# Hybrid encoder trunk: transposes, gating and split of the delta rule's output as a stage of their own ahead of w_out's products, and one gate chunk moved behind the Hyena norm

## Chip, cores and metric

The kernel runs on one core of a Trainium2 chip. The metric is the device time of one execution in microseconds. Five engines work side by side, each through an in-order queue of its own: TensorE (PE, matrix products), VectorE (DVE), ScalarE (ACT), GpSimd (POOL) and SyncE (SP, which issues nearly all the loads). Semaphores order the queues among each other.

## Reference

Two layers over 256 tokens of width 1024; all arrays are float32.

```python
for i in range(2):
    x = x + 0.5 * swiglu(rmsnorm(x), gate1, up1, down1)          # 1024 -> 2816 -> 1024
    q, k, v, z, beta, alpha, hy = split(rmsnorm(x) @ w_in)
    o_dn = rmsnorm_per_head(delta(q, k, v, ...) + flipped_delta(...)) * silu(z)   # 4 heads x 128
    o_hy = rmsnorm(x2 * longconv(x1 * longconv(v)))              # 512 channels
    x = x + concat([o_dn, o_hy]) @ w_out                         # 1024 x 1024
    x = x + 0.5 * swiglu(rmsnorm(x), gate2, up2, down2)
return rmsnorm(x)
```

The change touches the end of the mixer (the third to sixth line of the loop): the norm and the gate `silu(z)` of the delta rule's output, the Hyena norm, and the product with w_out.

## Kernel before

**Layout.** x is kept transposed: 8 tiles of 128 channels by 256 tokens. A feed-forward block walks over 22 steps of 128 hidden channels, each with three weight blocks of 512 KB (gate, up, down). The mixer makes its inputs in 28 chunks of 128 channels (`chunk`), the last four being the gate z.

**Split weights.** Products with the feed-forward weights and with w_out run in a reduced 32-bit format on operands that are split into a high and a low half. `load_w` lets SP load a block into a `raw` buffer (4 of them), ACT copies the high half into `wh` (3 buffers, line 179), DVE subtracts to give the low half `wl` (3 buffers, line 182). `split_act` does the same with activations (`yp`: ACT line 152, DVE line 153). `rank` multiplies one block of w_out (128 of its 1024 rows) by such a pair: three products for each of 8 output tiles, 24 in all, added into four PSUM banks (`acc`, tags c and d). The z chunks are not split: `load_raw` loads the weights, and a product of full float32 takes 8 products of two passes each. They read `yn`, a float32 copy of the normalised input, which lives in one `wl` and one `wh` buffer until the last chunk has read it.

**The end of the mixer, in program order.** Stage z makes the four gate tiles `zs` (`chunk(24 + i, ..., Silu)`, ACT line 530). Stage hn multiplies back the last long convolution (`py`), squares, sums (`st`), and ends with `hn.finish()`: `nv` (DVE), a power on POOL (`pw`, line 195), `dg` (DVE), `rbp` (PE), `rb` (ACT). Stage hw scales the Hyena rows by `rb` (`yn`, DVE line 942), splits them and runs `rank` on w_out's blocks 4 to 7. Stages solve and o finish the delta rule: products `ph`, then `po`; a sum of squares (`oss`), a power on POOL and a product on DVE give the normalised output `on` (line 960), one tile for each half of the tokens. Stage ow, for each of four heads, transposes the head's two 128 x 128 pieces into a PSUM tile `pot` (line 1002; tag b, 2 banks, shared with `st`, `rbp` and the z chunks' `pw`), gates it (`og`, DVE line 1004), splits it and runs `rank` on w_out's blocks 0 to 3. Stage ef loads and splits the first four weight blocks of the next feed-forward block (`early`; high half on ACT, low half on POOL, line 182), and `finish_resid` adds `acc` to x.

**What sets the order.** The program order is not the order on the engines. A planner goes through a modelled execution when the program is built, and on each engine takes, among the instructions that are ready, the one with the lowest place number. That is its place in the program, less an offset: `stage(name)` takes the offset from the table `PRM` (solve 800, o 800; z, hn, hw and ow have none; ef has -410), and some groups have one of their own inside a stage (`nfin` 350 in the norm's end, `feed` and `feedw` 300 for the loads and splits of weights, `evac` 2060). A tile also waits in the plan for a free buffer of its tag. The order that results is fixed; on the chip each engine keeps to it.

Of the kernel before, what the change touches and what calls it, by code (L numbers as in the profile page):

```python
# [55 lines left out]
PRM = { 'split': list(range(28, 36)),  # L56
 'y32': 300,
 'ah': [0, 0, 0],
 'av': 0,
 'ak': 0,  # L60
 'aq': 0,
 'gm_act': [1, 3],
 'e_lc': [0, 1, 0, 1, 0, 0, 0, 0, 0, 1],
 'e_both': [1, 1],
# [7 lines left out]
 'w1': 6,  # L72
 'sqp0': [1, 2, 4, 5, 7],
 'hold': 3,
 'ej': 0,
 'ea': ['S', 'e4', 'e2', 'e2', 'd2', 'd2', 'zg', 'ST'],
 'fj': 14,
# [12 lines left out]
def trunk_kernel(ctx: ExitStack, tc: tile.TileContext, xt, ffn, wba, win, wout, par, fpar, fwo, fnorm, con, feat, wnd, out):  # L90
# [10 lines left out]
    def pr(name):  # L101
        n = PRM.get(name, 0)
        return tc.high_priority(offset=n) if n else nullcontext()
# [6 lines left out]
    def stage(name):  # L110
        cur.close()
        cur.enter_context(pr(name))

    def psum(tag, name, shape=(128, 4, 128)):
        return ps.tile(list(shape), F32, tag=tag, name=name, bufs=2)

    def mm(o, l, r, start=True, stop=True, **kw):
        PE.matmul(o, lhsT=l, rhs=r, start=start, stop=stop, **kw)  # L118
# [24 lines left out]
    def behind(i, j):  # L143

        tc.add_manual_dep(i.ins, j.ins.name, mybir.DependencyInfo(mybir.DependencyClass.NoSync, mybir.DependencyReason.DATA), reason="order")

    def split_act(src, tag, bufs, scale=None, eng=V):

        pair = ap_.tile([128, 2, T], F32R, tag=tag + "p", name=tag + "p", bufs=bufs)
        hi, lo = pair[:, 0], pair[:, 1]  # L150
        if scale is None:
            A.activation(out=hi, in_=src, func=AF.Copy)  # L152
            eng.tensor_tensor(out=lo, in0=src, in1=hi.bitcast(F32), op=ALU.subtract)  # L153
        else:
            last[0] = A.activation(out=hi, in_=src, func=AF.Copy, scale=scale)
            last[1] = PRM["hold"]
            eng.scalar_tensor_tensor(out=lo, in0=src, scalar=scale, in1=hi.bitcast(F32), op0=ALU.mult, op1=ALU.subtract)  # L157
        return hi, lo, pair

    def cut(pieces, c):  # L160
        z = pieces[0].shape[1]
        return pieces[c.start // z][:, c.start % z:c.start % z + c.stop - c.start]

    def load_w(src, n=1024, eng=V, tag="", bufs=3, early=None):
        raw = wp.tile([128, n], F32, tag=tag + "raw", name="raw", bufs=bufs + (tag == ""))
        SP.dma_start(out=raw, in_=src)
        if early is None:
            hi = [wp.tile([128, n], F32R, tag=tag + "wh", name="wh", bufs=bufs)]
            lo = [wp.tile([128, n], F32R, tag=tag + "wl", name="wl", bufs=bufs)]
        else:  # L170
            t = [mx.tile([128, c], F32R, tag=g, name="early", bufs=b) for g, c, b in early]
            if len(t) == 1:
                t = [t[0][:, 0:1024], t[0][:, 1024:2048]]
            hi, lo = t[:len(t) // 2], t[len(t) // 2:]
        ns = max(len(hi), PRM["wsp"] if n == 1024 else 1)
        for i in range(ns):
            c = slice(i * n // ns, (i + 1) * n // ns)
            h, l_ = cut(hi, c), cut(lo, c)
            op = A.activation(out=h, in_=raw[:, c], func=AF.Copy)  # L179
            if last[1] > 0 and early is None and n == 1024:  # L180
                behind(op, last[0])
            eng.tensor_tensor(out=l_, in0=raw[:, c], in1=h.bitcast(F32), op=ALU.subtract)  # L182
        last[1] -= 1
        return hi, lo
# [109 lines left out]
    def accumulators(tags="aadd"):  # L294
        banks = [psum(t, "acc", (128, 2, T)) for t in tags]
        return [banks[m // 2][:, m % 2] for m in range(KD)]
# [19 lines left out]
    def load_raw(src):  # L316
        raw = wp.tile([128, 1024], F32, tag="raw", name="raw", bufs=4)
        SP.dma_start(out=raw, in_=src)
        return raw
# [5 lines left out]
    def rank32(acc, w, h, first, last):  # L325
        for m in range(KD):
            mm(acc[m], w[:, m * 128:(m + 1) * 128], h, start=(first and m % 2 == 0), stop=last, skip_group_check=True)
# [8 lines left out]
    def rank(acc, w, h, first, last):  # L336

        for m in range(KD):
            for i, (a, b) in enumerate(((0, 0), (1, 0), (0, 1))):
                mm(acc[m], cut(w[a], slice(m * 128, (m + 1) * 128)), h[b], start=(first and i == 0 and m % 2 == 0), stop=(last and i == 2),  # L340
                   skip_group_check=True)
# [161 lines left out]
    def bh(apc):  # L503

        return apc.unsqueeze(2).to_broadcast([128, 4, 128])

    def mixer(l, ys, norm, ab, wcols):
# [5 lines left out]
        def chunk(c, dst=None, func=AF.Copy):  # L513
            with pr("feed"):
                if early:
                    w = early.pop(0)
                else:
                    w = load_w(win[l, c]) if c in PRM["split"] else load_raw(win[l, c])
            p = psum("bc"[c % 2] if c < 4 else "b", "pw", (128, T))
            raw = ap_.tile([128, T], F32, tag="t1", name="raw_", bufs=7) if dst is None else dst  # L520
            if isinstance(w, tuple):
                proj(p, w, ys)
                with pr("evac"):
                    V.tensor_tensor(out=raw, in0=p, in1=norm.rb, op=ALU.mult)
                    if func != AF.Copy:
                        after(A.activation(out=raw, in_=raw, func=func), last_exp)
            else:
                proj32(p, w, yn)
                with pr("evac"):
                    i = A.activation(out=raw, in_=p, func=func)  # L530
                    if func != AF.Copy:
                        after(i, last_exp)
            return raw
# [41 lines left out]
        def tok(name, bufs):  # L575
            return [mx.tile([128, CW], F32, tag=name, name=name, bufs=bufs) for _ in range(2)]

        def d2(name):
            return mx.tile([128, 4, 128], F32, tag="d2", name=name, bufs=8)
# [130 lines left out]
        for a in range(2):  # L710
            for hp in (slice(0, 2), slice(2, 4)):
                p = psum("a", "gram", (128, 2, 2, 128))
                for i in range(2):
                    h = hp.start + i
                    mm(p[:, i], kq[:, h, 0, a * 128:(a + 1) * 128], kq[:, h, 0])
                for i in range(2):
                    h = hp.start + i
# [18 lines left out]
        for a in range(2):  # L736
            both, one = ((Ef0, Eb[0, 0]), (Eb1, Ef[1, 1]))[a]
            for hp in (slice(0, 2), slice(2, 4)):
                p = psum("d", "kqp", (128, 2, 2, 128))
                for i in range(2):  # L740
                    h = hp.start + i
# [8 lines left out]
        for q_ in range(4):  # L750
            t = d2("xm")
# [54 lines left out]
        for i in range(4):  # L806
            t = ap_.tile([128, T], F32, tag="hc", name="hv", bufs=4)
# [42 lines left out]
        for i in range(4):  # L850
            t = mx.tile([128, T], F32, tag="zs", name="vs", bufs=4)
# [4 lines left out]
        for a in range(2):  # L856
# [3 lines left out]
            t = d2("rho")  # L860
# [6 lines left out]
        for i in range(4):  # L867
            t = ap_.tile([128, T], F32, tag="hc", name="h1", bufs=4)
# [4 lines left out]
        z1 = tok("zt", 2)  # L873
# [38 lines left out]
        for i in range(4):  # L912
            t = ap_.tile([128, T], F32, tag="hc", name="x2", bufs=4)
# [2 lines left out]
        stage("z")  # L916

        zs = []
        for i in range(4):
            t = mx.tile([128, T], F32, tag="zs", name="zs", bufs=4)  # L920
            chunk(24 + i, t, AF.Silu)
            zs.append(t)

        stage("hn")
        hn = Norm(4, CW, "b")
        for i in range(4):
# [6 lines left out]
            V.tensor_tensor(out=xv, in0=py, in1=xv, op=ALU.mult)  # L933
            hn.add(x2[i])
        hn.finish()

        stage("hw")

        acc = accumulators("ccdd")
        for i in range(4):  # L940
            t = ap_.tile([128, T], F32, tag="t1", name="yn", bufs=7)
# [3 lines left out]
            else:  # L945
                with pr("feedw"):
                    w = load_w(wout[l, 4 + i])
# [10 lines left out]
        def tt(name, x, y, op):  # L958
            t = d2(name)
            V.tensor_tensor(out=t, in0=x, in1=y, op=op)  # L960
            return t
# [23 lines left out]
        for i in range(2):  # L985
# [9 lines left out]
            V.scalar_tensor_tensor(out=ss, in0=ss, scalar=1.0 / 128, in1=ssq[:, 4 * i:4 * i + 4], op0=ALU.mult, op1=ALU.add)  # L995
            f = rsqrt(ss, 4, f"of{i}")
            on.append(tt("on", po, bh(f), ALU.mult))
        stage("ow")
        for h in range(4):
            pt = psum("b", "pot", (128, T))  # L1000
            for i in range(2):
                PE.transpose(pt[:, i * 128:(i + 1) * 128], on[i][:, h], ident)
            t = ap_.tile([128, T], F32, tag="t1", name="og", bufs=7)
            V.scalar_tensor_tensor(out=t, in0=pt, scalar=P[:, C_DNN:C_DNN + 1], in1=zs[h], op0=ALU.mult, op1=ALU.mult)
            if 32 + h not in PRM["split"]:
                rank32(acc, load_raw(wout[l, h]), t, False, h == 3)
            else:
                with pr("feedw"):
                    w = load_w(wout[l, h])
                rank(acc, w, split_act(t, "y", 8), False, h == 3)  # L1010
        stage("ef")
        for _ in ahead([ffn[l, 1, j, i] for j in range(2) for i in range(2)], PRM["ma"]):
            pass
# [140 lines left out]
```

## Time and profile before

| | |
|---|---|
| median of 3 runs | 1235.63 us (1233.08 to 1235.89) |
| the profiled execution, its own time | 1238.01 us |
| span of the profiled execution, first to last instruction | 1236.2 us |
| mean granted clock of TensorE | 0.989 of 2.4 GHz |
| busy: PE, DVE, ACT, POOL | 1191.8, 867.8, 588.1, 304.8 us |
| transposes `pot`, first and last start | 393.8 and 1014.6 us |
| gate tiles `zs`, first and last start | 363.0 and 986.5 us |

The profile is of one execution. A start is counted from the span's first instruction; a row that says x4 merges four instructions that follow each other, with the time from the first start to the last end. Times in brackets behind a row are idle time of that engine just before it, with what ended it. PE's clock column is the granted share of 2.4 GHz. The two mixers lie at about 225 to 430 us and 830 to 1035 us of the span, with the same order of instructions.

### The profile page before, as it was taken

What the parts mean: (1) busy time and instruction counts of PE and PEld (TensorE: products, weight loads), DVE (VectorE), ACT (ScalarE), POOL (GpSimd) and SP (SyncE); (2) the same over time, 40 slices, a digit from 0 to 9 for tenths busy, and PEclk for the clock granted to TensorE, in tenths of its full rate; (3) what the DMA queues carried; (4) which work ended last, traced back from release to release, by engine and by line L of the source; (5) the groups of instructions that cost most, each with busy time, mean ns of one, the idle gap of its engine ahead of it and who ended that gap; (6) DMA issues with size and microseconds to landing.
All of it is one profiled execution on the core that took longest, in us unless ns stands there. A gap on an engine that the chain in (4) does not pass through costs nothing.

```text
span 1236.2 us, 20507 instructions
## 1 busy us (share of the span) xinstructions
PE 1191.8 (96%) x7908; PEld 1050.0 (85%) x7908; DVE 867.8 (70%) x1483; ACT 588.1 (48%) x1058; POOL 304.8 (25%) x254
## 2 busy tenths in 40 slices
PE   7999999999999899999999999999999989999996
PEld 5888888978878799999988888889888878999996
DVE  6876777658955566667778666776598665766665
ACT  5544555452333445555554445553523434555553
POOL 4122343211222411113231114331202234211111
PEclk9999999999999899999999999999999999999998
DMA  8555567113222445556635555750231324555551
GB/s 287 179 171 196 171 209 237 50 52 102 86 63 93 153 134 190 190 186 212 214 128 185 177 175 189 235 190 1 86 118 40 131 77 149 171 187 188 188 187 51
DMA packets 53912, 186.35 MB, mean 151 GB/s; under 512 B 6157, under 2 KB 7088, under 8 KB 53816
## 3 DMA queue, kind: packets, MB, share of 16 engines
q1 hardware_dynamic: 50156, 179.01, 43.9%
q10 hardware_dynamic: 3660, 6.05, 1.6%
q8 instruction: 62, 1.02, 0.3%
q14 instruction: 34, 0.28, 0.1%
HBM read 183.98 MB, written 1.05 MB: 150 GB/s over the span
## 4 chain that ended last, share of the span: by engine, by line
PE 71%; DVE 13%; DMA 8%; issue 3%; ACT 3%; POOL 1%; DVEq 0%; SPq 0%; ACTq 0%
PE acc L118 19%; PE u L118 15%; PE g L118 15%; PE pw L118 11%; DMA raw<-in_win 6%; DVE wl L182 4%; DMA raw<-in_ffn 2%; PE pe L118 1%; ACT wh L179 1%; PE pp L118 1%; PE py L118 1%; PE st L118 1%; DVE vs L552 1%; PE ph L118 1%; ACT early L179 1%
## 5 line engine op out<-in xcount | busy, mean ns | idle before, releaser
L182 DVE TENSOR_TENSOR wl<-raw,wh 128x1024 fp32r<-128x1024 f32 (+1 forms) x270 | 344.3, 1277 | 93.1 <-ACT wh L179 90.2
L179 ACT ACTIVATE wh<-raw 128x1024 fp32r<-128x1024 f32 (+1 forms) x270 | 282.0, 1047 | 121.6 <-PE acc L118 69.3
L118 PE MATMUL acc<-hp,wh 128*128 128x256 f32 x1408 | 265.9, 283 | 0.0
L118 PE MATMUL g<-yp,wh 128*128 128x512 f32 x656 | 245.2, 408 | 8.4 <-DVE yp L157 8.4
L118 PE MATMUL u<-yp,wh 128*128 128x512 f32 x656 | 237.6, 397 | 0.6 <-DVE ub L333 0.3
L118 PEld LDWEIGHTS acc<-hp,wh 128*128 128x128 f32 x1408 | 227.6, 191 | 3.6 <-issue 0.8
L368 POOL TENSOR_TENSOR sr<-gb,rb 128x256 f32<-128x256 f32 x88 | 110.2, 1253 | 451.4 <-ACT gb L366 451.4
L118 PE MATMUL acc<-hp,wl 128*128 128x256 f32 x704 | 194.5, 285 | 5.7 <-DVE wl L182 5.7
L118 PE MATMUL u<-yp,wl 128*128 128x256 f32 x656 | 169.9, 279 | 2.4 <-DVE wl L182 2.4
L118 PE MATMUL g<-yp,wl 128*128 128x256 f32 x656 | 172.0, 283 | 0.0
L118 PEld LDWEIGHTS g<-yp,wh 128*128 128x128 f32 x656 | 124.4, 190 | 40.2 <-DVE yp L157 9.5
L118 PE MATMUL pw<-y,raw 128*128 128x256 f32 x640 | 147.9, 380 | 0.0
L118 PEld LDWEIGHTS u<-yp,wh 128*128 128x128 f32 x656 | 124.1, 189 | 22.9 <-PE g L118 0.6
L118 PEld LDWEIGHTS acc<-hp,wl 128*128 128x128 f32 x704 | 133.5, 191 | 9.8 <-DVE wl L182 8.0
L118 PEld LDWEIGHTS pw<-y,raw 128*128 128x128 f32 x640 | 120.4, 191 | 24.7 <-issue 10.5
L118 PEld LDWEIGHTS u<-yp,wl 128*128 128x128 f32 x656 | 123.9, 189 | 10.6 <-DVE wl L182 3.7
L118 PEld LDWEIGHTS g<-yp,wl 128*128 128x128 f32 x656 | 124.9, 191 | 5.2 <-issue 1.4
L182 POOL TENSOR_TENSOR early<-raw,early 128x512 fp32r<-128x512 f32 (+1 forms) x44 | 74.6, 1709 | 115.3 <-ACT early L179 115.3
L332 ACT ACTIVATE gb<-g 128x256 f32<-128x256 f32 x88 | 33.3, 379 | 121.5 <-PE g L118 121.5
L153 DVE TENSOR_TENSOR hp<-ub,hp 128x256 fp32r<-128x256 f32 x88 | 56.8, 645 | 23.5 <-ACT hp L152 23.3
L333 DVE TENSOR_TENSOR gb<-g,gb 128x256 f32<-128x256 f32 x88 | 37.0, 420 | 45.4 <-ACT gb L332 45.4
L333 DVE TENSOR_TENSOR ub<-u,ub 128x256 f32<-128x256 f32 x88 | 37.0, 420 | 38.8 <-ACT ub L332 38.8
(436 smaller groups left out, 1632.4 us busy)
## 6 DMA issues: line engine op xcount, KB each, us to landing
raw<-in_ffn SPq DMA_DIRECT2D x264, 512.0 KB, 3.8
raw<-in_win SPq DMA_DIRECT2D x56, 512.0 KB, 4.2
raw<-in_wout SPq DMA_DIRECT2D x16, 512.0 KB, 4.4
w<-in_wnd ACTq DMA_DIRECT2D x16, 256.0 KB, 4.6
wo<-in_fwo ACTq DMA_DIRECT2D x8, 130.0 KB
X<-in_xt SPq DMA_DIRECT2D x4, 256.0 KB, 7.4
con_s<-in_con SPq DMA_DIRECT2D x1, 544.0 KB, 9.5
out<-X SPq DMA_DIRECT2D x2, 256.0 KB, 2.5
```

Of the source, the lines that this page charges most:

```text
L118: PE.matmul(o, lhsT=l, rhs=r, start=start, stop=stop, **kw)
L153: eng.tensor_tensor(out=lo, in0=src, in1=hi.bitcast(F32), op=ALU.subtract)
L179: op = A.activation(out=h, in_=raw[:, c], func=AF.Copy)
L182: eng.tensor_tensor(out=l_, in0=raw[:, c], in1=h.bitcast(F32), op=ALU.subtract)
L332: A.activation(out=t, in_=o[:, 1], func=AF.Copy)
L333: V.tensor_tensor(out=t, in0=o[:, 0], in1=t, op=ALU.add)
L368: G.tensor_tensor(out=sr, in0=sg, in1=norm.rb, op=ALU.mult)
L552: i = V.scalar_tensor_tensor(out=dst[:, lo:hi], in0=raw[:, lo + s_:hi + s_], scalar=P[:, w0 + j:w0 + j + 1], in1=dst[:, lo:hi], op0=ALU.mu ...
```

## The change

A new stage `og` with the offset 900 holds the transposes, the gating and the split of all four heads; the stage ow behind it holds only the loads and splits of w_out's blocks 0 to 3 and their products. The fourth z chunk (`PRM["z1"]` is 3) is written behind `hn.finish()` and so has a later place than the norm's instructions; it stands in stage hn, which has no offset. The branch for blocks that are not split falls away; `split` holds all eight, so it was not taken.

```diff
+ 'z1': 3, 'og': 900,
...
         zs = []
-        for i in range(4):
+        def gate(i):
             t = mx.tile([128, T], F32, tag="zs", name="zs", bufs=4)
             chunk(24 + i, t, AF.Silu)
             zs.append(t)
+
+        for i in range(PRM["z1"]):
+            gate(i)
 
         stage("hn")
         hn = Norm(4, CW, "b")
...
         hn.finish()
+        for i in range(PRM["z1"], 4):
+            gate(i)
...
-        stage("ow")
+        stage("og")
+        gated = []
         for h in range(4):
             pt = psum("b", "pot", (128, T))
             for i in range(2):
                 PE.transpose(pt[:, i * 128:(i + 1) * 128], on[i][:, h], ident)
             t = ap_.tile([128, T], F32, tag="t1", name="og", bufs=7)
             V.scalar_tensor_tensor(out=t, in0=pt, scalar=P[:, C_DNN:C_DNN + 1], in1=zs[h], op0=ALU.mult, op1=ALU.mult)
-            if 32 + h not in PRM["split"]:
-                rank32(acc, load_raw(wout[l, h]), t, False, h == 3)
-            else:
-                with pr("feedw"):
-                    w = load_w(wout[l, h])
-                rank(acc, w, split_act(t, "y", 8), False, h == 3)
+            gated.append(split_act(t, "y", 8))
+        stage("ow")
+        for h in range(4):
+            with pr("feedw"):
+                w = load_w(wout[l, h])
+            rank(acc, w, gated[h], False, h == 3)
```

## Rows read from the trace of the kernel before

**Rows 1.** The page: busy time of the engines, and the loads of w_out.

```profile
PE 1191.8 (96%) x7908; PEld 1050.0 (85%) x7908; DVE 867.8 (70%) x1483; ACT 588.1 (48%) x1058; POOL 304.8 (25%) x254
...
raw<-in_wout SPq DMA_DIRECT2D x16, 512.0 KB, 4.4
```

**Rows 2.** Windows: stretch, length, busy us of PE, PEld, DVE, ACT, POOL; clock.

```profile
395.10:408.50 13.40, 13.34 (x97) 13.20 (x98) 6.53 (x11) 4.37 (x7) 2.13 (x1) 0.87 0.24 79
...
416.10:428.90 12.80, 12.70 (x88) 12.50 (x88) 4.39 (x10) 4.89 (x10) 6.29 (x6) 0.83 0.52 183
...
1001.40:1013.30 11.90, 11.84 (x97) 11.71 (x98) 6.53 (x11) 4.37 (x7) 2.13 (x1) 1.00 0.27 88
1013.30:1020.80 7.50, 2.38 (x15) 1.51 (x13) 6.88 (x7) 4.18 (x7) 4.95 (x2) 0.80 0.41 129
1020.80:1033.30 12.50, 12.47 (x88) 12.27 (x88) 4.32 (x10) 4.83 (x10) 6.21 (x6) 0.85 0.53 184
...
416.10:420.20 4.10, 4.09 (x19) 4.09 (x20) 0.96 (x3) 0.22 (x1) 0.00 (x0) 0.50 0.71 285
```

**Rows 3.** Waits of PE, whole span: total us, times, longest.

```profile
PE acc L118 <- DVE yp L153: 7.1, 2, 3.6
...
PE acc L118 <- ACT yp L152: 4.1, 4, 1.2
...
PE pot L1002 <- DVE on L960: 1.4, 2, 0.7
...
PE pot L1002 <- DVE og L1004: 0.9, 2, 0.5
```

**Rows 4.** Timeline of PE, layer 1: start, length, instruction, idle before.

```profile
978.51 3.62 PE L118 MATMUL pw<-y,raw 128*128 128x256 f32 x16
...
984.55 1.89 PE L118 MATMUL pw<-y,raw 128*128 128x256 f32 x8
...
1000.12 0.41 PE L1002 MATMUL pot<-con_s,on 128*128 128x128 f32 x2 [0.72 <-DVE on L960]
1001.46 0.39 PE L118 MATMUL acc<-yp,wh 128*128 128x256 f32 x1 [0.93 <-ACT yp L152]
...
1013.26 0.38 PE L1002 MATMUL pot<-con_s,on 128*128 128x128 f32 x2
...
1020.81 0.80 PE L118 MATMUL acc<-yp,wh 128*128 128x256 f32 x2 [3.59 <-DVE yp L153]
```

**Rows 5.** Timeline of DVE, layer 1.

```profile
1002.13 1.43 DVE L153 TENSOR_TENSOR yp<-yn,yp 128x256 fp32r<-128x256 f32 x4
1004.46 0.69 DVE L960 TENSOR_TENSOR on<-po,pw__10161 128x512 f32<-128x512 f32 x1 [0.90 <-POOL pw__10161 L195]
1005.91 1.23 DVE L182 TENSOR_TENSOR wl<-raw,wh 128x1024 fp32r<-128x1024 f32 x1 [0.76 <-ACT wh L179]
...
1013.57 1.89 DVE L1004 SCALAR_TENSOR_TENSOR og<-pot,par_s,zs 128x256 f32<-128x256 f32 x4 [0.67 <-PE pot L1002]
1015.67 2.60 DVE L182 TENSOR_TENSOR wl<-raw,wh 128x1024 fp32r<-128x1024 f32 x1 [0.21 <-ACT wh L179]
1018.20 3.56 DVE L153 TENSOR_TENSOR yp<-og,yp 128x256 fp32r<-128x256 f32 x4
```

**Rows 6.** Timeline of POOL, layer 1.

```profile
1002.30 2.13 POOL L195 TENSOR_TENSOR pw__10161<-oss,mhalf 128x4 f32<-128x4 f32 x1 [3.05 <-DVE oss L995]
1014.82 2.37 POOL L182 TENSOR_TENSOR early<-raw,early 128x1024 fp32r<-128x1024 f32 x1 [10.40 <-ACT early L179]
1017.89 2.58 POOL L182 TENSOR_TENSOR early<-raw,early 128x1024 fp32r<-128x1024 f32 x1 [0.69 <-ACT early L179]
```

**Rows 7.** Timeline of ACT, layer 1.

```profile
986.76 1.05 ACT L179 ACTIVATE wh<-raw 128x1024 fp32r<-128x1024 f32 x1
```

**Rows 8.** Waits of all engines, 985 to 1035.

```profile
ACT wh L179 <- PE acc L118: 5.9, 3, 2.2
```

**Rows 9.** Waits of PE from 430 to 600 (the feed-forward block behind layer 0's mixer).

```profile
PE acc L118 <- DVE wl L182: 0.5, 1, 0.5
```

## Prediction

> **What bounds the kernel now.** I read the page first, then the busy time by stretch at the end of each mixer, then who waited for whom on TensorE (PE), then the timelines of PE, VectorE (DVE), GpSimd (POOL) and ScalarE (ACT) there. The page shows PE busy for 96% of the span [rows 1]: only what takes idle time or low clock from PE can move the end. In the feed-forward block behind a mixer PE waits once, for 0.5 us, in 170 us [rows 9], so a mixer that ends earlier hands its gain on to the last instruction.
>
> The idle time lies where the change lies. Call the delta rule's two normalised halves on0 and on1, the Hyena half of w_out hw0 to hw3, the delta half ow0 to ow3, and the four chunks of gate z0 to z3. Between the Hyena products and the delta products PE is busy for 2.38 of 7.50 us in layer 1 (layer 0 repeats it), and the delta products behind run at a mean granted clock of 0.83 and 0.85, with 0.50 (1.2 GHz of 2.4) in their first 4.1 us [rows 2]. The waits name the steps: 7.1 us in two waits for the gated tile's low half, 0.9 in two for a PSUM bank that `og` has to read out, 4.1 in four for a high half (two ahead of the Hyena products, 0.93 us each in layer 1's timeline, so 4.1 - 1.9 = 2.2 ahead of the delta products), 1.4 in two for on0 [rows 3, 4]. The timeline shows why: on1 leaves DVE at 1004.46 + 0.69 = 1005.15, but PE runs its transposes only at 1013.26, behind all 96 Hyena products [rows 4, 5]. Everything hangs on them: `og` 1.89 us for four, then w_out's third delta split (2.60), then the low halves (3.56), all in DVE's one queue, while PE stands for 3.59 us up to 1020.81 [rows 4, 5]. Dependencies alone would have let the transposes run eight us earlier.
>
> **Part one: transposes, gating and split as a stage of priority 900 ahead of w_out's products.** It removes and adds no instruction (16 transposes, 8 `og` and 8 splits stay); it moves them. With 900 they outrank the Hyena products, so as soon as on1 is there PE takes them between two products, and `og` and the halves have from 1005.2 to about 1013 for their work: 1.9 us of `og` and some 1.4 of subtractions on DVE (what Hyena's four took at 1002.13 [rows 5]), which lie under eight us of products. So these waits go: 7.1 + 0.9 + 2.2 = 10.2 us over both layers. With the idle time the low clock behind it should go. A Hyena stretch at full clock takes 11.90 us for 96 products [rows 2], so 88 take 10.9; they took 12.80 and 12.50, a loss of 1.9 + 1.6 = 3.5 us. Sum 13.7.
>
> What it may cost. First, PE's queue is in order: a transpose that the planner puts earlier than on1 comes stops the Hyena products. No row shows this. Below it is nothing (on1 is planned behind the low halves in DVE's queue anyway), above it is 3.7 us a layer (1005.15 less the first Hyena product at 1001.46). The planner may well take the power on POOL for shorter than the 2.13 us it had there [rows 6], since that one met DVE's subtractions; I take 0.5 a layer, 1.0 in all. Second, the splits of ow2 and ow3 cannot come earlier than now: ACT's `wh` waits for the products that free its buffer, 5.9 us in three waits [rows 8]. With a Hyena start near 1000.3, PE is through ow0 at about 1000.3 + 11.9 + 1.2 (transposes) + 2.9 = 1016.3; 1.05 on ACT and 1.25 on DVE make ow3 ready at 1018.7, due at 1022.3. Cover 3.6 us, and POOL's split of the next block's weights, which now meets this work, takes 2.37 and 2.58 a piece [rows 5, 6]. Between nothing and 2.6 a layer; nearest is the split that took 2.60 instead of 1.2, a loss of 1.4 that the cover holds: I take 0.4, 0.8 in all.
>
> The row of that split bears a rule: it started 0.85 us into a POOL instruction of 2.37 and ended 1.08 us behind its end, and the four low halves behind it took 3.56 where Hyena's four took 1.43, with POOL's next 2.58 us across their start [rows 5, 6]. The Trainium skill, in "SBUF — State Buffer", section "Who interferes with whom", says that a DVE instruction with two SBUF inputs and a GpSimd instruction that reads SBUF exclude each other for the whole of whichever came first. The trace agrees. By that rule the gating's subtractions gain by leaving POOL's neighbourhood, but w_out's last splits stay in it and may become the wait; that is the second rival below.
>
> **Part two: z3 behind the Hyena norm's sums.** z3 is 16 records of 0.226 us: half of the 16 at 978.51 and the 8 at 984.55 [rows 4], 3.6 us. Its gate on ACT moves with it, and its load, which SP still issues ahead of w_out's. It can fill what PE now waits at the norm: 1.4 for on0 and 1.9 for the first high halves, 3.3 us in both layers [rows 3, 4]. In the place it leaves, the norm's products (already queued behind it) move up. The first half may stay where it is, since it filled a wait there; the 8 records of 1.89 us suffice for 1.65 a layer, but the planner need not lay them on the chip's gap. Between 0 and 3.3 I take 2.4. In layer 0 the clock fell behind that gap (13.40 against 11.90 us for the same products), in layer 1 behind an equal gap it did not [rows 2]; of 1.5 I take half, 0.7.
>
> What z3 holds: `yn` sits in one of three `wh` and one of three `wl` buffers until its last product, and hw2's split, at 986.76 right behind z3's gate [rows 7], must now wait for it: 1.05 on ACT and 1.23 on DVE near 1001 to 1004. I cost it at nothing: hw0 and hw1 cover it with 48 products, 5.9 us. Without that cover it is up to 2.3 a layer, later one to one for each us that z3 ends behind 1005. z3's raw buffer, too, comes free some 13 us later, so one or two of w_out's loads do (4.4 us each by the page [rows 1]); they are due for the split after 1010 and arrive by 1009.
>
> **Downstream.** The next block's early weights lose the same 8 us of lead. The first two are split on POOL by 1017.2 and 1020.5 [rows 6], before a mixer end near 1025.5; the other two are used only in the second of its 22 steps. I add nothing.
>
> **Sum**: 13.7 + 2.4 + 0.7 - 1.0 - 0.8 = 15.0 us. The profiled execution took 1238.0 (span 1236.2, 1.8 around it), 2.4 above the median of the runs, 1235.6; a saving of 15 gives 1223.0 in a profile and 1220.6 as a median. I say 1220.5.
>
> **The rivals.** One: it does nothing. The planner's clock may bring on1 so late that the transposes stay behind the Hyena products, and z3 may stay in its old gap. Against it: PE took on0's two transposes at 1000.12, the moment they came, without any priority [rows 4]. Then 1235.6, or up to 2 less: 1234.5.
>
> Two: a wait takes the place of the one removed. Either on1's transposes stop the Hyena products for 2 to 3.7 us, or ow2's and ow3's splits meet POOL's two instructions of 2.4 and 2.6 and come late by more than the cover. For it: the split at 1015.67 shows the meeting, and ACT holds an early weight's split, itself waiting for a load, in front of w_out's. Against: the cover of 3.6 us. About 2.5 us and one fall of the clock, 1.6, a layer: 15.0 - 8.2 = 6.8 saved, 1228.8.
>
> Three, on the other side: on1's transposes are planned ahead of all Hyena products. PE then waits for on1 (3.7 us), z3 is no filler but 3.6 us of work laid in front of those products, its old place goes to waits in the solve chain, and one more stretch of low clock costs 1.7: 9.0 a layer against the 6.9 that part one gives. Then 2 x 2.1 slower: 1239.8. It breaks even where the first Hyena product comes 6.9 us later than now, and is a measurable loss from 8.8. For it: priority 900 stands above solve and o (800) too; against: on1 needs on0's and the norm's steps on DVE and POOL first, which also feed the Hyena products.
>
> **Chances.** The forecast (1216 to 1224.5) 0.66; two (1224.5 to 1231.9) 0.18; one 0.08; three 0.06; below 1216 0.02. The lowest that the terms allow is all gains and no cost: 10.2 + 3.5 + 3.3 + 1.5 = 18.5, 1217.1, with 2 us for what the planner shifts elsewhere 1215. The range runs from 1215 to 1231 and leaves out one, three and both ends, some 0.18. 0.3% is 3.7 us, about what a measurement of this kernel can tell from no change: faster 0.86, same 0.08, slower 0.06.
>
> **What the new profile shows.** Right: transposes of on1 amid the Hyena products, near 1005; no wait for a gated half; clock 1.00 through both halves; the first FFN product some 7 to 8 us earlier in layer 0 and 14 to 16 in layer 1. z3's records between the sums and the first Hyena product. Wrong: a wait of PE for `on` of over 1.5 us, for `wl` among the delta products, or z3 at its old place. The forecast fails most likely if the planner, from the new places, orders a stretch elsewhere worse, which no row of before can show.

## The result and the profile after

The changed kernel takes 1220.42 us (median of five runs) against 1235.89 of the kernel before, timed beside it: a ratio of 0.986, 95% interval 0.984 to 0.988, or 15.5 us less. The forecast was 1220.5. One of the five runs took 5115.78 us, against 1217.04 to 1222.47 for the others, and is left out of the ratio; the median of the four is 1219.05. The profiled execution took 1217.7 us, 20.3 less than the one before.

The page of the changed kernel, busy time of the engines (answers to [rows 1]):

```profile
PE 1183.9 (97%) x7908; PEld 1043.6 (86%) x7908; DVE 870.7 (72%) x1483; ACT 589.8 (49%) x1058; POOL 307.1 (25%) x254
```

The number of instructions is the same on each engine. PE is busy 7.9 us less with the same 7908 products; 7.0 of that lies in the two stretches of the Hyena and delta products (55.0 us of PE before, 48.1 now), where the clock was low before. The rest of the saving is idle time.

Windows of the changed kernel over the end of both mixers, with the columns of [rows 2]: z3 and the norm, the Hyena half, the delta half, the first steps of the feed-forward block (first layer 0, then layer 1):

```profile
387.50:392.10 4.60, 4.60 (x28) 4.17 (x28) 3.72 (x10) 2.48 (x6) 1.47 (x2) 1.00 0.02 4
392.10:404.20 12.10, 12.10 (x103) 12.07 (x102) 9.14 (x15) 6.16 (x9) 1.50 (x1) 1.00 0.52 173
404.20:416.20 12.00, 11.99 (x100) 11.79 (x99) 6.68 (x7) 6.84 (x10) 7.05 (x4) 1.00 0.62 203
416.20:437.40 21.20, 19.84 (x117) 17.14 (x118) 16.59 (x26) 11.00 (x25) 12.37 (x13) 1.00 0.39 134
983.00:987.70 4.70, 4.70 (x29) 4.25 (x28) 3.74 (x10) 2.48 (x6) 1.57 (x2) 1.00 0.01 3
987.70:999.70 12.00, 12.00 (x102) 11.99 (x101) 9.03 (x15) 6.16 (x9) 1.48 (x1) 1.00 0.57 177
999.70:1011.80 12.10, 12.07 (x101) 11.86 (x99) 7.22 (x8) 7.21 (x11) 7.45 (x5) 1.00 0.60 205
1011.80:1032.70 20.90, 19.92 (x118) 17.22 (x119) 16.29 (x26) 10.64 (x24) 12.02 (x12) 1.00 0.40 133
```

PE has no gap from z3 to the last delta product and the clock stands at 1.00 throughout; before, the stretch between the halves held 5.1 idle us of 7.50, and the clock 0.50 to 0.87 in five of six rows [rows 2]. Only the last stretch of a layer has idle time left, 1.4 and 1.0 us.

Waits of PE in the changed kernel, layer 1 from 975 to 1030 (answers to [rows 3]):

```profile
PE st L119 <- POOL sq L239: 0.8, 2, 0.6
PE g L119 <- DVE yp L158: 0.4, 1, 0.4
```

The four waits of [rows 3] do not occur, here or elsewhere in the span: none for `on`, for `og`, or for a half of `yp` ahead of w_out's products. In their place stand three small ones. Two are in the feed-forward block: 0.57 us for `sq`, the squares of its norm, and 0.4 for `yp`, its input. The other wait for `sq`, 0.27 us, is for the Hyena norm's squares.

Timeline of PE in the changed kernel, layer 1 (answers to [rows 4]):

```profile
983.81 0.61 PE L119 MATMUL rbp<-dg,con_s 128*128 128x128 f32 x4
984.26 3.62 PE L119 MATMUL pw<-y,raw 128*128 128x256 f32 x16
987.71 0.27 PE L1009 MATMUL pot<-con_s,on 128*128 128x128 f32 x1
987.74 0.36 PE L119 MATMUL acc<-yp,wh 128*128 128x256 f32 x1
...
991.41 0.38 PE L1009 MATMUL pot<-con_s,on 128*128 128x128 f32 x2
...
1012.19 0.71 PE L119 MATMUL g<-yp,early 128*128 128x512 f32 x3 [0.42 <-DVE yp L158]
...
1016.31 0.61 PE L119 MATMUL st<-con_s,sq 128*128 128x1 f32 x4 [0.57 <-POOL sq L239]
```

All 16 records of z3 now lie between the norm's sums and the first Hyena product, and the transposes lie one or two at a time between Hyena products.

**Where the time came from.** Three starts are counted from one, the landmark, that comes ahead of all that the change moves, DVE's `S<-ppq 64x256` (365.24 in layer 0, 960.82 in layer 1). A is the first Hyena product, B the first feed-forward product, C the first product with a hidden block (`acc<-hp`), one step on. Each cell has layer 0 and layer 1; the last column is C, both layers, against the kernel before. e1 to e11 are the runs below.

| | A | B | C | C against before |
|---|---|---|---|---|
| before | 28.58, 28.58 | 62.38, 60.54 | 81.60, 79.77 | |
| after | 26.92, 26.92 | 51.70, 51.37 | 72.04, 71.70 | -17.63 |
| e1 part one alone | 28.58, 28.58 | 54.27, 53.29 | 74.33, 73.37 | -13.67 |
| e2 part two alone | 26.92, 26.92 | 58.84, 60.13 | 78.00, 79.35 | -4.02 |
| e3 offset 0 | 26.91, 26.92 | 59.95, 60.25 | 79.12, 79.48 | -2.77 |
| e4 products behind on1 | 29.96, 29.96 | 55.86, 54.74 | 75.91, 74.77 | -10.69 |
| e5 early low halves set to zero | 26.91, 26.92 | 51.15, 51.15 | 70.38, 70.38 | -20.61 |
| e6 early blocks behind the input | 26.92, 26.92 | 51.15, 51.15 | 77.16, 77.14 | -7.07 |
| e7 two z chunks behind | 28.95, 28.95 | 53.42, 53.85 | 73.47, 73.90 | -14.00 |
| e8 two early low halves on DVE | 26.92, 26.92 | 51.71, 51.59 | 70.86, 70.74 | -19.77 |
| e9 four | 26.92, 26.92 | 51.40, 51.79 | 70.55, 70.94 | -19.88 |
| e10 one | 26.92, 26.92 | 51.35, 51.40 | 70.83, 70.84 | -19.70 |
| e11 the changed kernel again | 26.91, 26.92 | 51.60, 52.18 | 71.89, 72.50 | -16.98 |

The change gives 3.32 us up to A, 16.53 between A and B, and takes 2.22 back between B and C: 20.34 and 20.33 us where the kernel before takes 19.22 and 19.23. The remaining 2.7 of the 20.3 us between the two profiled executions lie ahead of the first landmark (1.3), between layer 0's C and the second landmark (1.2) and behind layer 1's C (0.2); the first landmark lies between 363.6 and 367.7 us in these profiles, so I put them down to the difference between one execution and another.

### The profile page after: what moved, and what is told of

It is laid out like the page before. It is cut to its first block, busy times and chain, and to the rows that moved or that the text cites. A ratio compares the mean times of both kernels' runs of the same rounds, so it can differ in the third digit from the quotient of the medians.

```text
span 1215.9 us, 20509 instructions
## 1 busy us (share of the span) xinstructions
PE 1183.9 (97%) x7908; PEld 1043.6 (86%) x7908; DVE 870.7 (72%) x1483; ACT 589.8 (49%) x1058; POOL 307.1 (25%) x254
## 4 chain that ended last, share of the span: by engine, by line
PE 69%; DVE 13%; DMA 9%; ACT 4%; issue 3%; POOL 1%; SPq 0%; DVEq 0%; ACTq 0%
PE acc L119 17%; PE u L119 15%; PE g L119 15%; PE pw L119 11%; DMA raw<-in_win 6%; DVE wl L183 4%; DMA raw<-in_ffn 3%; PE pe L119 1%; ACT wh L180 1%; PE pp L119 1%; PE py L119 1%; PE st L119 1%; ACT early L180 1%; DVE vs L553 1%; PE po L119 1%
## 5 line engine op out<-in xcount | busy, mean ns | idle before, releaser
L183 DVE TENSOR_TENSOR wl<-raw,wh 128x1024 fp32r<-128x1024 f32 (+1 forms) x270 | 349.2, 1295 | 81.6 <-ACT wh L180 78.4
L119 PEld LDWEIGHTS pw<-y,raw 128*128 128x128 f32 x640 | 120.1, 190 | 24.9 <-issue 10.5
```

## The experiments

**Each part alone.** e1 has the new stage and all four z chunks in their old place; e2 has z3 moved and the old stage ow.

```diff
# e1
- 'z1': 3, 'og': 900,
+ 'z1': 4, 'og': 900,
# e2
-        stage("og")
-        gated = []
+        stage("ow")
...
-            gated.append(split_act(t, "y", 8))
...
+                rank(acc, w, split_act(t, "y", 8), False, h == 3)
```

> Part one alone: the og stage with offset 900, all four z chunks ahead of the norm as before. Theory (the parts add, each works in its own gap): the waits for the gated halves and the bank go (10.2 us) with the low clock behind them (3.5), the two waits at the norm (3.3) stay: 1236 - 13.7 = about 1222, TensorE waits about 0.7 for on and 0.9 for a high half in each layer. Rival (z3 as filler is what lets the transposes in without a stop): the transposes stop the Hyena products, 1227 or more.

> Part two alone: z3 behind the norm's sums, transposes, gating and split per head inside the ow stage as before. Theory (z3 fills the waits at the norm): the first Hyena product comes about 1.6 us earlier in each layer, the waits behind the Hyena products stay: 1236 - 3.3 = about 1232.5, or 1231 if layer 0 also keeps its clock. Rival (the gain of 15 came from re-planning, z3 alone is worth nothing): 1236.

Measured: e1 1223.54 us, ratio 0.990 (0.987 to 0.992); e2 1233.14, 0.998 (0.996 to 0.999). In the table e1 gives 13.67 and e2 4.02, which make 17.69 where both together give 17.63: the parts add up. Waits of PE in e1, whole span:

```profile
PE acc L119 <- ACT yp L153: 1.9, 2, 0.9
PE pot L1009 <- DVE on L966: 1.4, 2, 0.7
```

These are the 3.3 us at the norm, which part one leaves. Waits of PE in e2, whole span:

```profile
PE acc L119 <- DVE yp L154: 6.1, 2, 3.3
PE acc L119 <- ACT yp L153: 3.5, 2, 1.8
PE pot L1008 <- DVE og L1010: 0.7, 2, 0.4
```

These are the other half, the waits between the Hyena and the delta products, 10.3 us where [rows 3] give 10.2. Windows of e2 from A to B, layer 0 and layer 1:

```profile
393.40:425.30 31.90, 26.40 (x202) 25.27 (x200) 17.34 (x23) 13.63 (x22) 12.67 (x9) 0.89 0.51 168
998.20:1031.40 33.20, 28.18 (x201) 27.01 (x199) 17.39 (x23) 13.57 (x22) 12.72 (x9) 0.85 0.51 167
```

The same products take 1.8 us longer in layer 1, at a lower mean clock. That is why part two alone keeps 3.60 us in layer 0 and only 0.42 in layer 1 at C: the 1.66 gained at A is there in both, and low clock behind the gap that stayed took most of it in layer 1.

e1 also repeats the riddle of [rows 2]. Windows of e1 behind the gap of 1.65 us that stands ahead of the Hyena products, layer 0 and layer 1:

```profile
396.00:400.00 4.00, 4.00 (x28) 4.00 (x27) 1.03 (x3) 1.06 (x1) 0.87 (x1) 0.75 0.00 0
994.00:998.00 4.00, 4.00 (x35) 3.87 (x34) 2.33 (x6) 1.33 (x2) 2.11 (x1) 1.00 0.00 0
```

The same idle pieces (0.72 and 0.93) stand in both layers; the clock falls in layer 0 only, and in layer 1 it stays at 1.00 through both halves.

**The stage without its offset.** e3 keeps the new order of the program and takes the 900 away.

```diff
- 'z1': 3, 'og': 900,
+ 'z1': 3, 'og': 0,
```

> As the changed kernel, but the og stage has no offset (place numbers behind those of the Hyena products). Theory (the offset moves the transposes, the stage by itself does not): the planner puts seven of a layer's transposes behind the Hyena products again, time as in part two alone, 1231 to 1233. Rival (it is enough that w_out's loads and splits stand behind all four gatings in the program): 1222 or less.

Measured: 1232.82 us, ratio 0.998 (0.996 to 0.999). Timeline of PE in e3, layer 0:

```profile
391.30 0.27 PE L1009 MATMUL pot<-con_s,on 128*128 128x128 f32 x1
402.92 0.49 PE L1009 MATMUL pot<-con_s,on 128*128 128x128 f32 x3
403.77 0.83 PE L1009 MATMUL pot<-con_s,on 128*128 128x128 f32 x4 [0.36 <-DVE og L1011]
406.41 0.58 PE L119 MATMUL acc<-yp,wh 128*128 128x256 f32 x1 [1.81 <-ACT yp L153]
411.16 0.79 PE L119 MATMUL acc<-yp,wh 128*128 128x256 f32 x2 [2.68 <-DVE yp L154]
```

Seven of eight transposes run behind the Hyena products, and both waits are back. Written as a stage of its own, but with the place number of the text, part one gains nothing over part two alone (2.77 us at C against 4.02); the offset is what moves the transposes. The offset on the old stage, without the new one, was not run.

**Rival three forced.** e4 writes the Hyena products behind the stage og and orders the first block's behind the first head's two transposes, so that PE must wait for on1.

```diff
-                rank(acc, w, split_act(t, "y", 8), i == 0, False)
+                hyena.append((w, split_act(t, "y", 8)))
...
+            first_t = last_t if h == 0 else first_t
+        for i, (w, y) in enumerate(hyena):
+            rank(acc, w, y, i == 0, False, first_t if i == 0 else None)
```

> As the changed kernel, but the first Hyena product is ordered on TensorE behind the transposes of on1 for the first head (the third rival of the prediction, made to happen); nothing else is waited for. Theory (an in-order queue pays the wait in full): on1 leaves VectorE 2.2 us behind the place of the first Hyena product, with the transposes some 2.5 to 3 us a layer, plus 1.5 to 1.9 where the clock falls: 1220.4 + 5 to 9, so 1225 to 1229. Rival (the stretch behind makes up for it, since w_out's splits set its end): 1222 or less.

Measured: 1226.51 us, ratio 0.992 (0.989 to 0.994). Waits of PE in e4, whole span:

```profile
PE pot L1012 <- DVE on L969: 2.6, 2, 1.3
```

A comes 3.04 us later a layer than in the changed kernel, C 3.47 on the mean. So the wait of rival three can be had, and costs 3 of the 3.7 us a layer that the timelines gave for it. The kernel stays faster than before all the same: of the rival's 9.0 us a layer only this wait and some low clock (0.58 for 4 us in layer 0, none in layer 1) came, less than part one gives.

**One more z chunk behind the sums.** e7 moves z2 too.

```diff
- 'z1': 3, 'og': 900,
+ 'z1': 2, 'og': 900,
```

> As the changed kernel, but two z chunks, z2 and z3, behind the norm's sums: 7.2 us of products where 3.6 left no wait. Theory (only the waits at the norm are worth filling; the solve chain now waits in the place that z2 leaves, and hw2's split waits longer for the buffers of yn): the first Hyena product comes 1 to 3.6 us later than with one chunk, 1223 to 1228. Rival (the more filler the better): 1217 to 1219.

Measured: 1223.06 us, ratio 0.990 (0.988 to 0.992). A comes 2.03 us later a layer than with one chunk. One chunk takes away all the idle time ahead of the Hyena products, 1.66 us a layer. The second, of the same length, finds no wait left there, and where it stood PE now waits 0.4 us for `er` and 0.3 for `uf` in layer 1; the rest of the 2.03 was not traced.

**Where the 2.2 us are given back.** Timelines of the changed kernel, layer 1. DVE:

```profile
1002.16 2.64 DVE L183 TENSOR_TENSOR wl<-raw,wh 128x1024 fp32r<-128x1024 f32 x1 [2.38 <-ACT wh L180]
1005.54 2.62 DVE L183 TENSOR_TENSOR wl<-raw,wh 128x1024 fp32r<-128x1024 f32 x1 [0.73 <-ACT wh L180]
...
1014.07 4.87 DVE L158 SCALAR_TENSOR_TENSOR yp<-X,par_s,yp 128x256 fp32r<-128x256 f32 x6
```

POOL:

```profile
1001.31 2.41 POOL L183 TENSOR_TENSOR early<-raw,early 128x1024 fp32r<-128x1024 f32 x1 [12.13 <-ACT early L180]
1004.63 2.44 POOL L183 TENSOR_TENSOR early<-raw,early 128x1024 fp32r<-128x1024 f32 x1 [0.92 <-ACT early L180]
1009.20 5.44 POOL L183 TENSOR_TENSOR early<-raw,early 128x512 fp32r<-128x512 f32 x4 [2.12 <-ACT early L180]
1014.59 0.79 POOL L231 TENSOR_TENSOR sq<-X 128x256 f32<-128x256 f32 x1
```

ACT:

```profile
1008.49 2.42 ACT L180 ACTIVATE early<-raw 128x512 fp32r<-128x512 f32 x4 [2.99 <-DMA raw<-in_ffn]
```

POOL in the kernel before, layer 1:

```profile
1026.33 5.58 POOL L182 TENSOR_TENSOR early<-raw,early 128x512 fp32r<-128x512 f32 x4 [5.86 <-ACT early L179]
1032.38 0.61 POOL L230 TENSOR_TENSOR sq<-X 128x256 f32<-128x256 f32 x1 [0.46 <-DVE X L286]
```

The splits of ow2 and ow3 meet two POOL subtractions and take 2.64 and 2.62; they end at 1004.80 and 1008.16, in time. But the third and fourth early block come last: ACT takes them at 1008.49 behind a wait of 2.99 us for their load, POOL ends at 1014.64, and only then come the squares of the next norm, for which PE waits at 1016.31. In the kernel before POOL was through with the same four pieces by 1031.91 and ran its first square at 1032.38, ahead of the first feed-forward product (1033.42).

e5 takes POOL's reading away: it writes zeros for the low halves of the four early blocks, so the low parts of these weights are left out of the products.

```diff
-            eng.tensor_tensor(out=l_, in0=raw[:, c], in1=h.bitcast(F32), op=ALU.subtract)
+            (G.memset(l_.bitcast(F32), 0.0) if nolo else eng.tensor_tensor(out=l_, in0=raw[:, c], in1=h.bitcast(F32), op=ALU.subtract))
```

> As the changed kernel, but GpSimd fills the low halves of the four early blocks of each mixer with zeros and reads nothing for it (their low parts are left out of the next block's first two steps). From the first FFN product to the first down product the changed kernel takes 20.5 us a layer, the kernel before 19.4. Theory (GpSimd's reads of these blocks now meet VectorE's preparation of the next block, and w_out's last two splits, which took 2.6 instead of 1.2): the splits take 1.25, the six low halves about 4.2 instead of 4.87, the stretch comes back to 19.4, the time to about 1218. Rival (ScalarE's early halves, which wait for their loads ahead of the first halves of the next block, set it): the stretch stays at 20 or more.

Measured: 1215.62 us, ratio 0.984 (0.982 to 0.986). Timelines of e5, layer 1. DVE:

```profile
988.63 1.22 DVE L183 TENSOR_TENSOR wl<-raw,wh 128x1024 fp32r<-128x1024 f32 x1
...
1001.01 1.23 DVE L183 TENSOR_TENSOR wl<-raw,wh 128x1024 fp32r<-128x1024 f32 x1 [2.43 <-ACT wh L180]
...
1012.31 4.18 DVE L158 SCALAR_TENSOR_TENSOR yp<-X,par_s,yp 128x256 fp32r<-128x256 f32 x6
```

POOL:

```profile
987.95 1.92 POOL L183 MEMSET early<- 128x512 f32 x4
```

The splits of ow2 and ow3 fall from 2.6 to 1.23 us, the input's low halves from 4.87 to 4.18, and B to C takes 19.23 us again. The zeros wait for no load, so they are written long before (the last by 989.87) and POOL is idle beside these two splits; e5 takes away both the reading and the late place in POOL's queue. The split at 988.63 is the one that runs beside a write. The Trainium skill ("SBUF — State Buffer", "Who interferes with whom") says that a DVE instruction with two SBUF inputs contends with a GpSimd instruction that reads SBUF, not with one that only writes it. The trace agrees: 2.62 across a subtraction on POOL, 1.22 beside the writing of zeros.

e6 orders the split of the third and fourth early block behind the split of the input on ACT.

```diff
-        for _ in ahead([ffn[l, 1, j, i] for j in range(2) for i in range(2)], PRM["ma"]):
+        for _ in ahead([ffn[l, 1, 0, i] for i in range(2)], PRM["ma"][:2]):
...
+        for _ in ahead([ffn[l, 1, 1, i] for i in range(2)], PRM["ma"][2:], last[0]):
```

> As the changed kernel, but the split of the third and fourth early block is ordered behind the preparation of the next block on ScalarE (and so behind the squares on GpSimd). Theory (these splits in front of the preparation cost the 1.1 us a layer): the first FFN product comes up to 0.5 us earlier, the stretch behind it takes 19.4, the time about 1217.5 to 1218.5. Rival (the second step then waits for its weights): the stretch takes 21 or more, 1222 or more.

Measured: 1230.72 us, ratio 0.996 (0.994 to 0.997). Waits of PE in e6 from 410 to 460:

```profile
PE u L119 <- DVE ub L336: 2.8, 1, 2.8
```

B comes 0.55 and 0.22 us earlier, as the blocks no longer stand in front of the input, but B to C takes 26.0 us. The rival held in its size. That the second step's weights come late is read from the order and not from a named wait: POOL ends the last of their low halves 11.1 us behind B in layer 1, and the wait that the trace names is for `ub`, DVE's reading of a `u` product out of PSUM, which frees the bank for the next one.

**Low halves of the early blocks on DVE.** DVE idles 2.38 us ahead of ow2's split and 0.73 ahead of ow3's (above). e10, e8 and e9 let it subtract the first, the first two and all four low halves of the mixer's early blocks in POOL's place; e11 is the changed kernel again, timed on the same chip.

```diff
-    def ahead(srcs, slots):
+    def ahead(srcs, slots, engs=(G,) * 8):
...
-            early.append(load_w(src, eng=G, early=SLOT[t]))
+            early.append(load_w(src, eng=engs[i], early=SLOT[t]))
...
+        for _ in ahead([ffn[l, 1, j, i] for j in range(2) for i in range(2)], PRM["ma"], (V, V, G, G)):
```

The last line is e8's; e9 has `(V, V, V, V)` and e10 `(V, G, G, G)`.

> The changed kernel with one thing different: the low halves of the first two early blocks of the mixer's end are subtracted on VectorE, those of the third and fourth stay on GpSimd. The theory that GpSimd's subtractions and VectorE's splits of w_out hold each other up: VectorE does the two early ones in about 1.25 us each between its own splits, which fall from 2.6 to about 1.25, so the raw buffers come free over a microsecond earlier and the third and fourth early block arrive earlier. Normalised input of the feed-forward block earlier by 0.2 to 0.5 us, first product to first down product 19.5 to 20.2 us against 20.5: 1.0 to 2.5 us less than the changed kernel over both layers. Rival: the plan now lays an early split, which waits for its load and for ScalarE, in front of w_out's third split on VectorE's queue, and w_out's products wait for it: slower than the changed kernel by up to 3 us.

> As before, with the low halves of all four early blocks on VectorE, those of the third and fourth in two pieces each. The theory: nothing on GpSimd stands across VectorE's subtractions any more, so the six low halves of the feed-forward input take 4.2 us again and not 4.9; but the four pieces (about 0.65 us each, 2.6 us) lie in VectorE's queue ahead of the residual sum, and wait there for loads that land at about 5.4 us behind w_out's last block. If these loads are late, the residual sum waits behind them and the feed-forward block begins 1 to 3 us later a layer: slower than with two. Rival: they land in time, and the whole 3 us come back that were found when GpSimd read nothing.

> As before, with the low half of the first early block alone on VectorE. GpSimd then meets one split of w_out and not two. The theory of the two engines gives about half of what two blocks give, 0.5 to 1.5 us over both layers; if the gain comes from the order of the loads alone, one block gives nothing.

> The changed kernel itself, beside the three variants on the same chip: 1220.4 us, ratio 0.986 to the kernel before. The variants are to be held against this run.

Measured, all against the same runs of before (1236.43): e8 1217.03 us, 0.985 (0.983 to 0.987); e9 1217.19, 0.985 (0.983 to 0.987); e10 1217.44, 0.986 (0.984 to 0.988); e11 1218.39, 0.986 (0.984 to 0.988). The medians are 1.0 to 1.4 us under e11, less than the intervals can tell. The table can: all three come 2.1 to 2.3 us earlier at C than the changed kernel's first profile, 2.7 to 2.9 than its second, and they have it from B to C, which takes 19.15 us in e8 and e9 and 19.48 and 19.44 in e10. Timelines of e8, layer 1. DVE, the split of ow2:

```profile
1002.54 1.22 DVE L183 TENSOR_TENSOR wl<-raw,wh 128x1024 fp32r<-128x1024 f32 x1
```

POOL in e8:

```profile
1007.15 5.06 POOL L183 TENSOR_TENSOR early<-raw,early 128x512 fp32r<-128x512 f32 x4 [17.74 <-ACT early L180]
1012.17 0.79 POOL L231 TENSOR_TENSOR sq<-X 128x256 f32<-128x256 f32 x1
```

DVE and POOL in e10:

```profile
1004.96 2.58 DVE L183 TENSOR_TENSOR wl<-raw,wh 128x1024 fp32r<-128x1024 f32 x1 [1.56 <-ACT wh L180]
...
1013.52 5.00 DVE L158 SCALAR_TENSOR_TENSOR yp<-X,par_s,yp 128x256 fp32r<-128x256 f32 x6
```

```profile
1006.77 5.89 POOL L183 TENSOR_TENSOR early<-raw,early 128x512 fp32r<-128x512 f32 x4 [0.30 <-ACT early L180]
1012.61 0.80 POOL L231 TENSOR_TENSOR sq<-X 128x256 f32<-128x256 f32 x1
```

My reason for them held in its size and not in its place. In e10 one split of w_out still takes 2.58 and the input's low halves 5.00, longer than in the changed kernel, and nearly the whole gain is there. So these two are not what gives the time back, and B does not come earlier beyond what two profiles of one kernel differ by. What all three share is POOL's queue: it is through with the early blocks by 1012.21 (e8) and 1012.66 (e10) instead of 1014.64, so the squares start 2.7 and 1.4 us earlier by the landmarks, and PE's wait for them is gone.

The late squares reach PE in a second way too. Waits of PE's weight loads (PEld) from 1013 to 1032 in the changed kernel:

```profile
PEld st L119 <- POOL sq L239: 0.9, 1, 0.9
PEld u L119 <- DVE ub L334: 0.3, 1, 0.3
```

The same in e7, 1017 to 1037:

```profile
PEld u L119 <- DVE ub L334: 0.8, 1, 0.8
```

DVE's splits of the next three weight blocks in layer 1, in the changed kernel:

```profile
1018.86 4.57 DVE L183 TENSOR_TENSOR wl<-raw,wh 128x1024 fp32r<-128x1024 f32 x3
```

In the kernel before:

```profile
1039.01 3.48 DVE L182 TENSOR_TENSOR wl<-raw,wh 128x1024 fp32r<-128x1024 f32 x3
```

The 0.9 and 0.3 make the 1.2 us by which B to C is longer than in e8, where neither wait occurs. In e1, e4 and e7 the first square starts as late as in the changed kernel (2.4 us behind B; before, 1.0 ahead of it), but PE's weight loads wait for the squares 0.2 us or not at all; B to C takes 20.04 to 20.08 all the same, with 0.7 to 0.8 of waiting for `ub`. By the order of the queues that wait hangs on DVE: of its next three splits the two that start while POOL works on the squares take 1.75 us instead of 1.21, and the norm's `nv`, which follows them, starts 11.5 us behind B in all four of these kernels. Its sums had then been through for 1.5 to 1.8 us, and DVE came to it without a pause: its own queue held it. It starts 10.5 behind B in e10, where the three splits take 3.48 again and the wait for `ub` is 0.3, and 9.0 to 9.2 in the kernel before, e8 and e9. So slowed subtractions on DVE have a share after all, one stage later than I looked for them. How the 1.2 us divide between the squares that PE waits for and DVE's slowed queue, no run separates.

Why one block is enough can be read but was not tried alone: the raw buffer of the first early block comes free at 1002.26 in e10 (1001.03 + 1.23 on DVE) and at 1003.72 in the changed kernel (POOL), and ACT takes the third early block at 1006.06 instead of 1008.49 (0.6 of each difference is the landmark's). That DVE would hold the residual sum behind late loads in e9 does not show at B.

## Why the prediction was right

The time, the direction and both mechanisms came as forecast; the sum of 15.0 us came out at 17.63 in the profile's landmarks, and stays within the interval of the medians (1 - 0.988 to 1 - 0.984 of 1235.9 us, 15 to 20 us). Term by term:

- **Part one, 13.7**: 15.36 at B (A to B falls from 33.80 and 31.96 to e1's 25.69 and 24.71), 13.67 at C, behind its own share of the 2.2 us given back. The transposes run amid the Hyena products as the dependencies said, and every wait named went. I had counted the idle time and the low clock of the 88 products behind it, and not that of the eight products and eight transposes inside the gap: 15 records of products and transposes took 2.38 us there [rows 2], while now 102 records take 12.00, so 15 take 1.76. That is 0.6 a layer, most of the 1.66 that the term was too small by.
- **Cost of on1 in PE's queue, 1.0**: nothing. PE has no wait for `on`; e4 shows what it would be, 3.0 a layer.
- **Cost of the splits of ow2 and ow3, 0.8**: nothing. They took 2.6 each, as bounded, and the cover held both; no delta product waits for `wl`.
- **Part two, waits 2.4 of 3.3**: all of it, 1.66 a layer. The planner laid z3 exactly on the chip's gap, so the doubt was not needed. The split of hw2 stood under its cover as costed.
- **Part two, layer 0's clock, 0.7 of 1.5**: A to B falls by 0.91 more than in e1 in layer 0, and by 0.26 in layer 1: 1.17.
- **Downstream, "I add nothing"**: the step that failed. It costs 2.22. I checked that the first two early blocks come in time and that the other two are used late, and both is true; but I did not ask what is queued behind them on POOL. It is the squares of the next norm. They start 2.4 us behind B instead of 1.0 ahead of it; PE's weight loads wait 0.9 us a layer for them, and 0.3 for `ub`, which comes behind DVE's splits that the squares slow. e8 to e10, whose B is that of the changed kernel within some 0.4 us, have 2.1 to 2.3 us back with POOL relieved of one, two or four subtractions. That POOL's late queue is the cause is shown by this; the shares of its two ways to PE are not.

So the sum came near because its errors had both signs: terms too small by 3.05 (1.66 + 0.92 + 0.47), costs of 1.8 that did not come, and 2.2 given back that was not seen. 3.05 + 1.8 - 2.22 = 2.63, which is 17.63 less 15.0. That the median came within 0.1 us of the forecast is luck: the four runs beside the long one spread over 5 us, and e11, the same kernel, gave 1218.39. The first feed-forward product came 10.68 us earlier in layer 0 and 19.85 in layer 1, counted from the landmarks, where I had said 7 to 8 and 14 to 16: that sign was missed on the high side.

Of the rivals, one is refuted by the transposes' place, and e3 shows the kernel in which it would have held. Two is refuted in the form I gave it: the meeting with POOL's subtractions took place and was covered, and the wait that did come was one stage later and smaller (1.1 a layer instead of 4.1). Three is refuted by A, and by e4 in its price.

## What to carry to other kernels

When an engine idles for an input whose producers have long been done, look in the queues for the instruction that stands in front of them; here two transposes stood behind 96 products, and the new program text did not move them without its place number (e3). Filling a gap ends where the gap does: one chunk moved behind the sums gave all 1.66 us a layer, a second cost 2.03. When a stage ends earlier, list what each engine still has queued from work that hung on the old time (here loads, splits and then squares on POOL), and what stands behind that on the other engines, for there the next wait lies.

## What the runs showed of the hardware

- After equal gaps of PE (0.72 + 0.93 us) the granted clock fell to 0.50, which is 1.2 GHz, for some three us in layer 0 (mean 0.52 from 396.4 to 399.8 in the kernel before, 0.75 from 396 to 400 in e1) and stayed at 1.00, 2.4 GHz, in layer 1, in both kernels. What makes the difference stays open. Behind the larger gap of e2 PE was busy for 26.40 us in one layer and 28.18 in the other with the same products.
- A subtraction of two SBUF tiles of 128x1024 on DVE takes 1.21 to 1.23 us with POOL idle, beside a POOL instruction that only writes (e5), and, in the changed kernel, in all 84 cases where it started ahead of the POOL instruction that it met. Where POOL had started first, it took 1.75 us across a square and 2.08 to 2.64 across a subtraction.
